# Hybrid block on one core: the compressed branch's transposition first in each group, its product behind the first unit

## The chip, the cores and the metric

The kernel runs on one NeuronCore of a Trainium2 chip. The metric is the device time of one execution in microseconds (us). Below, TensorE is the matrix engine (PE in the trace, with PEld for its weight loads), ScalarE is ACT, VectorE is DVE, GpSimd is POOL, SyncE is SP.

## What is computed

One transformer block of 512 tokens and width 1024: an mLSTM branch and a sparse attention branch side by side, then an output projection, a convolutional feed-forward part, a gated embedding and a last norm. The change lies in the sparse attention, where each query takes the gated sum of three softmax branches:

```python
# per group g of 4 heads, per block of queries
s_c = einsum(q, Kc) - slope * dist_c;  p_c = softmax(s_c)      # compressed keys: 31 of them
o_c = einsum(p_c, Vc)
o_s = einsum(softmax(q Ksel - ...), Vsel)                      # selected blocks: all 512 positions
o_w = einsum(softmax(q Kwin - ...), Vwin)                      # window: all 512 positions
return g0 * o_c + g1 * o_s + g2 * o_w
```

The sums over keys may be taken in any order, so the compressed branch may come anywhere among the others.

## The kernel before

Every product of two float32 matrices is made of three in a faster form: a value is split into a rounded part and the rest (hi and lo), and hi*hi, lo*hi and hi*lo are added in PSUM.

The attention stage runs over eight *groups* (g, i): g is one of two sets of four heads, i one of four blocks of 128 queries, in the order (0,3), (0,2), (0,1), (0,0), (1,0), (1,1), (1,2), (1,3). `scores` (lines 698 to 756) makes, for one head, the scores on TensorE (tile s), their exponentials on ScalarE (line 747) and the gated probabilities on VectorE and GpSimd (lines 755 and 753). For the two long branches they stand in E, queries by keys; for the compressed branch the four heads of a group share Ec, 128 queries by 4 x 32 keys.

A group's values are worked off in *units* (`value_units`, line 758): one for each 128 keys of a long branch, so 2(i+1), and one for the compressed branch. `CPOS` = (1, 2, 2, 2) (line 32) sets the place of the latter: second in the groups with i = 0, third in the others. The main loop (lines 814 to 843) does for each unit:

- `value_turn`: TensorE turns the probabilities of the four heads into a PSUM tile pt, keys by queries (line 780: four transpositions of 128 x 128). ScalarE copies it into ph, the hi part (line 783), and VectorE takes the rest into pl (line 784). pt, ph and pl have two buffers each.
- For the compressed unit there is one transposition (line 771), since the four heads lie side by side in Ec. Its outcome has head r in rows 32r to 32r+31, so four ScalarE copies of 32 x 128 (line 774) bring the heads side by side into rows 0 to 31 of the one tile phc, and four VectorE subtractions of 32 x 128 (line 777) put the rest into rows 32 to 63.
- The products of the unit *before* (`value_product`): two of 128 x 512 (lines 788 and 790) into the group's sum pv, or for the compressed unit a single one, of phc (line 788 too).
- Scores of the next group, one head after another, and `st.fill(FILL1)`: 0.9 us, by the plan's own estimates, of *filler*, which is a projection that needs nothing of the attention (pmo, pmq: 24 products of 128 x 512 each; later poa, the output projection).

Behind a group's last product `value_end` copies half of pv on ScalarE (os, line 794), adds the halves on VectorE (ao, line 797), and splits the sum into mixa (lines 803 and 804). The output projection poa (lines 411, 412, 415) multiplies mixa; its first two of four input blocks are group set g = 0, the others g = 1.

`st.spend` only moves the plan's clock, by which a few later steps are put in. The text order is not the last word: a scheduler reorders the instructions of each engine by its own estimates when the program is built, and the engines then run their queues strictly in that order.

Of the kernel before, what the change touches and what calls it, by code (L numbers as in the profile page):

```python
# [11 lines left out]
AF = mybir.ActivationFunctionType  # L12
# [16 lines left out]
T_GATES = 8.0  # L29
T_CT = 8  # L30
T_CS = 3.0
CPOS = (1, 2, 2, 2)
NSC = (0, 2)
HO = (2, 2, 2, 3)
T_NS = 3.2
# [26 lines left out]
def f32(ap):  # L62
    return ap.bitcast(F32)
# [3 lines left out]
def hybrid_block_kernel(ctx: ExitStack, tc: tile.TileContext, a, out):  # L67
    nc = tc.nc
    TE, VE, SE, GE = nc.tensor, nc.vector, nc.scalar, nc.gpsimd
# [8 lines left out]
    def bank(tag, bufs, n, name):  # L78
        shape = [128, 512] if n == 1 else [128, n, 512]
        return psum.tile(shape, F32, tag=tag, bufs=bufs, name=name)  # L80
# [10 lines left out]
    def pT(name):  # L91
        return bank("T", 2, 1, name)

    def pV(name):
        return bank("V", 1, 1, name)
# [137 lines left out]
    st = Stream()  # L233
# [3 lines left out]
    ident, negm = cols[:, C_ID:C_ID + 128], cols[:, C_NEG:C_NEG + 128]  # L237
# [109 lines left out]
    def first_split(k):  # L347
        g = xbuf[:, k, S:S + 1]
        SE.activation(xh[:, k], xbuf[:, k, 0:S], AF.Copy, scale=g)
        raw = s1raw[min(k, k // 2 * 2) if k > 1 else k]  # L350
        raw = raw[:, k % 2 if k > 1 else 0]
        for c0, c1 in (((0, 288), (288, W1)) if k == 0 else ((0, W1),)):
            i = SE.activation(hi1[:, k % 6, c0:c1], raw[:, c0:c1], AF.Copy)
        VE.scalar_tensor_tensor(xl[:, k], xbuf[:, k, 0:S], g, f32(xh[:, k]), op0=ALU.mult, op1=ALU.subtract)
        for c0, c1 in (((0, 288), (288, W1)) if k == 0 else ((0, W1),)):
            VE.tensor_sub(lo1[:, k % 6, c0:c1], raw[:, c0:c1], f32(hi1[:, k % 6, c0:c1]))
        return i
# [10 lines left out]
    for k in range(KB):  # L368
        last = first_split(k)
# [58 lines left out]
    Vc = apool.tile([128, 2, 128], F32R, name="Vc")  # L428
    phc = apool.tile([128, 512], F32R, name="phc")
# [266 lines left out]
    Ec = {}  # L696
# [61 lines left out]
    def value_units(g, i):  # L758
        n = (i + 1) * 128
        units = []  # L760
        for br in range(2):
            for kt in range(i + 1):
                units.append((br * n + kt * 128, V[:, kt, 2 * br + g]))
        units.insert(CPOS[i], (None, Vc[:, g]))
        return units

    def value_turn(g, i, Es, u, unit):
        c0, vs = unit
        pt = pT(f"pt{g}{i}_{u}")
        if c0 is None:  # L770
            TE.transpose(pt[:, 0:128], Ec.pop((g, i)).rearrange("p r n -> p (r n)"), ident)
            for r in range(4):
                src, sl = pt[32 * r:32 * r + 32, 0:128], slice(r * 128, (r + 1) * 128)
                SE.activation(phc[0:32, sl], src, AF.Copy)
            for r in range(4):
                src, sl = pt[32 * r:32 * r + 32, 0:128], slice(r * 128, (r + 1) * 128)
                VE.tensor_sub(phc[32:64, sl], src, f32(phc[0:32, sl]))
            return phc, None
        for r in range(4):
            TE.transpose(pt[:, r * 128:(r + 1) * 128], Es[r][:, c0:c0 + 128], ident)  # L780
        ph = main.tile([128, 512], F32R, tag="PH", bufs=2, name=f"ph{g}{i}_{u}")
        pl = main.tile([128, 512], F32R, tag="PL", bufs=2, name=f"pl{g}{i}_{u}")
        SE.activation(ph, pt, AF.Copy)  # L783
        VE.tensor_sub(pl, pt, f32(ph))  # L784
        return ph, pl

    def value_product(pv, vs, ph, pl, first, last):
        TE.matmul(pv, vs, ph, start=first, stop=False)  # L788
        if pl is not None:
            TE.matmul(pv, vs, pl, start=False, stop=last)  # L790

    def value_end(g, i, pv):
        os = t2k(f"os{g}{i}")
        SE.activation(os[0:64], pv[64:128], AF.Copy)
        ao = t2k(f"ao{g}{i}")
        for par in range(2):
            VE.tensor_add(ao[par * 64:(par + 1) * 64, 0:256].rearrange("p (b n) -> p b n", b=2),
                          pv[0:64].rearrange("p (b o n) -> p o b n", b=2, o=2)[:, par],
                          os[0:64].rearrange("p (b o n) -> p o b n", b=2, o=2)[:, par])
        aov = ao[:, 0:256].rearrange("p (b n) -> p b n", b=2)  # L800
        dh = mixa[:, 0, 2 * g:2 * g + 2, i * 128:(i + 1) * 128]
        dl = mixa[:, 1, 2 * g:2 * g + 2, i * 128:(i + 1) * 128]
        SE.activation(dh, aov, AF.Copy)
        VE.tensor_sub(dl, aov, f32(dh))
# [9 lines left out]
    for x, (g, i) in enumerate(groups):  # L814
        nxt = groups[x + 1] if x + 1 < len(groups) else None
        if nxt and nxt[0] != g:
            st.until("q11")
        units = value_units(g, i)
        nu = len(units)
        pv = None  # L820
        Ns = []
        for u in range(nu):
            got = value_turn(g, i, Es, u, units[u])
            st.spend(0.43)
            if pend:
                pend()
                st.spend(0.43)
            if u == 0:
                pv = pV(f"pv{g}{i}")

            def product(u=u, got=got, g=g, i=i, pv=pv, vs=units[u][1], last=(u == nu - 1)):
                value_product(pv, vs, *got, u == 0, last)
                if last:
                    value_end(g, i, pv)
            pend = product
            if nxt:
                while len(Ns) * nu < 4 * (u + 1):
                    st.fill(FILL0)
                    Ns.append(scores(*nxt, len(Ns)))
                    st.spend(score_cost[nxt[1]])  # L840
            st.fill(FILL1)
        Es = Ns
# [488 lines left out]
```

## Time and profile before

| | us |
|---|---|
| median of 3 runs (lowest, highest) | 641.08 (640.48, 641.81) |
| the profiled execution | 639.04 |
| its span, first to last instruction | 637.2 |
| TensorE busy in the span | 618.9 |
| VectorE busy | 426.6 |
| ScalarE busy | 314.1 |
| attention's value stage, about 103 to 244 us | 141 |

The profile gives one execution: for every instruction its engine, its start and how long it was under way, and for every idle stretch which instruction ended it. Products on TensorE overlap: one of 128 x 512 is shown as 0.39 us long, while the next starts 0.23 us after it. A wait thus shows as idle time only from 0.16 us up; by the starts it is seen whole.

### The profile page before, as it was taken

The numbers are of one execution on the slowest core, as the hardware profiler recorded it, in microseconds if no ns is written. First come the engines' busy times: TensorE is split into PE (matmuls) and PEld (weight loads), VectorE is DVE, ScalarE is ACT, GpSimd is POOL, SyncE is SP. The second block draws the span as 40 slices with busy tenths as digits, with TensorE's granted clock in tenths as the row PEclk, the third lists the DMA queues.
The fourth block names the chain that finished last, engine by engine and source line by source line (L and its number), as shares of the span: only waits on it lengthen the run. The fifth ranks groups of instructions, "written<-read, shape, count | busy, mean of one in ns | idle before, by whom it ended". The sixth has DMA issues, their size and how long they took to land. (4 is left out here: it accounts for less than half of the span.)

```text
span 637.2 us, 8437 instructions
## 1 busy us (share of the span) xinstructions
PE 618.9 (97%) x3013; PEld 498.4 (78%) x3013; DVE 426.6 (67%) x882; ACT 314.1 (49%) x656; POOL 36.6 (6%) x85
## 2 busy tenths in 40 slices
PE   9997999999999999999999999999999999999994
PEld 6886877777777777777878888888888888888884
DVE  6898648888878977784786555565656444445476
ACT  7457445677656756555555334343333323233254
POOL 0400005211111200000000000000000000000000
PEclk9999999999999999999999999999999999999999
DMA  8702034211121153013233333333222233534703
GB/s 327 288 22 96 14 120 121 79 34 38 63 67 33 34 199 99 34 34 99 67 99 100 100 99 100 99 100 97 93 88 93 93 100 100 143 120 135 195 3 133
DMA packets 22921, 63.02 MB, mean 99 GB/s; under 512 B 2712, under 2 KB 7192, under 8 KB 22812
## 3 DMA queue, kind: packets, MB, share of 16 engines
q1 hardware_dynamic: 21344, 59.92, 28.8%
q0 software_dynamic: 1248, 2.16, 1.5%
q8 instruction: 24, 0.39, 0.3%
q10 hardware_dynamic: 288, 0.41, 0.2%
q14 instruction: 17, 0.14, 0.1%
HBM read 56.71 MB, written 2.10 MB: 92 GB/s over the span
## 5 line engine op out<-in xcount | busy, mean ns | idle before, releaser
L1080 ACT ACTIVATE u<-zv 128x512 fp32r<-128x512 f32 x16 | 10.1, 633 | 45.3 <-DVE zv L1078 45.3
L1077 DVE TENSOR_TENSOR zv<-pu,n2rb 128x512 f32<-128x512 f32 x16 | 11.1, 691 | 31.3 <-PE pu L415 31.3
L783 ACT ACTIVATE ph<-pt 128x512 fp32r<-128x512 f32 x40 | 23.5, 598 | 16.9 <-PE pt L780 16.3
L784 DVE TENSOR_TENSOR pl<-pt,ph 128x512 fp32r<-128x512 f32 x40 | 27.0, 684 | 6.6 <-ACT ph L783 6.0
L753 POOL TENSOR_SCALAR E<-E,rr 128x512 f32<-128x512 f32 (+3 forms) x32 | 21.2, 663 | 158.1 <-DVE rr L750 111.8
L1067 DVE TENSOR_TENSOR zg<-pu,n2rb 128x512 f32<-128x512 f32 x16 | 11.1, 692 | 26.0 <-PE pu L415 24.6
L780 PE MATMUL pt<-cols,E 128*128 128x128 f32 x160 | 27.7, 274 | 0.4 <-DVE E L755 0.3
L780 PEld LDWEIGHTS pt<-cols,E 128*128 128x128 f32 x160 | 20.0, 140 | 7.1 <-DVE E L755 2.6
L1107 DVE TENSOR_TENSOR X<-pd,X 128x512 f32<-128x512 f32 x8 | 5.5, 692 | 29.6 <-PE pd L415 29.6
L1070 ACT ACTIVATE cv<-zg,cols 128x512 f32<-128x512 f32 x16 | 13.1, 816 | 20.1 <-DVE zg L1067 20.1
L1073 ACT ACTIVATE cv<-cv 128x512 f32<-128x512 f32 x16 | 10.1, 631 | 24.6 <-DVE cv L1072 24.6
L747 ACT ACTIVATE E<-s,nm 128x384 f32<-128x384 f32 (+2 forms) x48 | 22.2, 473 | 0.0
L788 PE MATMUL pv<-ph,V 128*128 128x512 f32 x40 | 18.7, 468 | 0.4 <-ACT ph L783 0.4
L1081 DVE TENSOR_TENSOR u<-zv,u 128x512 fp32r<-128x512 f32 x16 | 11.1, 692 | 10.5 <-ACT u L1080 10.5
L790 PE MATMUL pv<-pl,V 128*128 128x512 f32 x40 | 16.7, 416 | 0.0
L737 DVE TENSOR_REDUCE nm<-s 128x2 f32<-128x768 f32 (+2 forms) x24 | 16.3, 681 | 0.0
L1066 POOL MEMSET zg<- 128x2 f32 x16 | 1.5, 100 | 244.0 <-DVE cv L1072 151.0
L261 DVE TENSOR_TENSOR acc<-acc,sq 128x512 f32<-128x512 f32 x21 | 14.4, 684 | 0.1
L964 PEld LDWEIGHTS mo<-vo,mw 128*128 128x128 f32 x80 | 11.4, 191 | 2.1 <-issue 0.7
L755 DVE TENSOR_SCALAR E<-E,rr 128x512 f32<-128x512 f32 (+3 forms) x32 | 13.0, 405 | 0.1
L749 DVE RECIPROCAL rr<-rs 128x3 f32<-128x3 f32 x32 | 5.5, 171 | 11.1 <-ACT E L747 11.1
L747 ACT ACTIVATE Ec<-s,nm 128x32 f32<-128x32 f32 x24 | 6.9, 286 | 11.8 <-DVE nm L737 11.6
(1102 smaller groups left out, 2017.6 us busy)
## 6 DMA issues: line engine op xcount, KB each, us to landing
X<-in_xg SPq DMA_DIRECT2D x1, 2048.0 KB, 8.5
xo<-xturn SPq DMA_DIRECT2D x32, 64.0 KB, 2.1
wgr<-in_w_pg SPq DMA_DIRECT2D x4, 512.0 KB, 4.6
s1r<-in_w_s SPq DMA_DIRECT2D x3, 672.0 KB, 9.2
xT<-in_xg SPq DMA_DIRECT2D x3, 514.0 KB, 8.3
rawx<-in_cmp_w SPq DMA_DIRECT2D x3, 512.0 KB, 6.2
Q<-hlq POOLq DMA_DIRECT2D x12, 128.0 KB, 3.3
out_y<-xo SPq DMA_DIRECT2D x3, 512.0 KB, 2.6
```

Source lines behind the costliest of these rows:

```text
L261: return VE.tensor_add(acc[:, :n], acc[:, :n], sq[:, :n])
L737: VE.tensor_reduce(out=nm[:, 1:3], in_=sw, axis=AX.X, op=ALU.max, negate=True)
L747: SE.activation(e, p, AF.Exp, bias=nm[:, b:b + 1], accum_out=rs[:, b:b + 1])
L753: GE.tensor_scalar(e, e, rr[:, b:b + 1], 0.0, op0=ALU.mult, op1=ALU.add)
L755: VE.tensor_scalar(e, e, rr[:, b:b + 1], None, op0=ALU.mult)
L780: TE.transpose(pt[:, r * 128:(r + 1) * 128], Es[r][:, c0:c0 + 128], ident)
L783: SE.activation(ph, pt, AF.Copy)
L784: VE.tensor_sub(pl, pt, f32(ph))
L788: TE.matmul(pv, vs, ph, start=first, stop=False)
L790: TE.matmul(pv, vs, pl, start=False, stop=last)
L964: TE.matmul(po[:, 0:130], Ws[j][:, (i - j) * 128:(i - j + 1) * 128], vones(j, h), start=(j == 0), stop=(j == i))
L1070: SE.activation(cv, zg[:, 2:S + 2], AF.Identity, scale=cw(2), bias=cols[:, C_CB + f:C_CB + f + 1])
```

## The change

The compressed branch is no unit any more. `CPOS` and its unit are gone, so a group has one unit fewer. A new step, `c_turn`, does its transposition, its four copies and its four subtractions ahead of the group's first unit. The one product of phc with Vc follows the first unit's two products. No instruction is added, dropped or altered in size; the plan's clock is moved by 0.11 and 0.23 us for the moved steps, and eight `st.fill(FILL1)` fall away in the text, so that filler is taken later.

```diff
-CPOS = (1, 2, 2, 2)
...
-        units.insert(CPOS[i], (None, Vc[:, g]))
         return units
+
+    def c_turn(g, i):
+        pt = pT(f"pt{g}{i}_c")
+        TE.transpose(pt[:, 0:128], Ec.pop((g, i)).rearrange("p r n -> p (r n)"), ident)
+        for r in range(4):
+            src, sl = pt[32 * r:32 * r + 32, 0:128], slice(r * 128, (r + 1) * 128)
+            SE.activation(phc[0:32, sl], src, AF.Copy)
+        for r in range(4):
+            src, sl = pt[32 * r:32 * r + 32, 0:128], slice(r * 128, (r + 1) * 128)
+            VE.tensor_sub(phc[32:64, sl], src, f32(phc[0:32, sl]))
...
-        if c0 is None:
-            TE.transpose(pt[:, 0:128], Ec.pop((g, i)).rearrange("p r n -> p (r n)"), ident)
...
-            return phc, None
...
+        c_turn(g, i)
+        st.spend(0.11)
         for u in range(nu):
             got = value_turn(g, i, Es, u, units[u])
...
                 value_product(pv, vs, *got, u == 0, last)
+                if u == 0:
+                    TE.matmul(pv, Vc[:, g], phc, start=False, stop=False)
+                    st.spend(0.23)
```

What becomes of the engines' queues, at the two places that matter. In the names, pt01_0 is unit 0 of group (0,1), pt01_c the compressed transposition, E2_1 the probabilities of head 2 in query block 1.

TensorE at the start of group (0,1), before:

```order
L780 MATMUL pt01_0_1558<-cols_73,E0_1_1364 128x128
L780 MATMUL pt01_0_1558<-cols_73,E1_1_1413 128x128
L780 MATMUL pt01_0_1558<-cols_73,E2_1_1466 128x128
L411 MATMUL pmo3_1538<-x1h_119,mo3h_1383 128x512
L412 MATMUL pmo3_1538<-x1l_120,mo3h_1383 128x512
L788 MATMUL pv02_1351<-ph02_6_1548,V_309 128x512
L780 MATMUL pt01_0_1558<-cols_73,E3_1_1518 128x128
L730 MATMUL s0_0_1580<-K_308,Q0_560 128x320
L732 MATMUL s0_0_1580<-K_308,Q0_560 128x320
L734 LDWEIGHTS identb_114
L734 MATMUL s0_0_1580<-maskt_115,identb_114 128x2x128
L790 MATMUL pv02_1351<-pl02_6_1549,V_309 128x512
```

and with the change, from the compressed transposition to the group's first product:

```order
L767 MATMUL pt01_c_1540<-cols_73,Ec01_1372 128x128
L779 MATMUL pt01_0_1550<-cols_73,E0_1_1370 128x128
L779 MATMUL pt01_0_1550<-cols_73,E1_1_1409 128x128
L779 MATMUL pt01_0_1550<-cols_73,E2_1_1471 128x128
L779 MATMUL pt01_0_1550<-cols_73,E3_1_1509 128x128
L411 MATMUL pmo3_1597<-x1l_120,mo3h_1426 128x512
L410 MATMUL pmo3_1597<-x1h_119,mo3h_1426 128x512
L411 MATMUL pmo3_1597<-x1l_120,mo3h_1426 128x512
L410 MATMUL pmo3_1597<-x1h_119,mo3h_1426 128x512
L787 MATMUL pv01_1568<-ph01_0_1555,V_309 128x512
```

The transpositions of unit 0 were spread over the end of the group ahead; now all five stand together behind it, four filler products follow, and then the first product, which needs ph01_0. Groups (0,3), (1,2) and (1,3) have the same five and four filler products; (1,0) has a mask product more; (1,1) has three fillers, a score product and two masks; (0,2) five fillers and two masks; (0,0) eight fillers.

ScalarE at the same place, before:

```order
L747 ACTIVATE E3_1_1518,rs3_1_1519<-s3_1_1509,nm3_1_1508 128x256 x2
L577 ACTIVATE vo_886<-vo_886 128x512
L783 ACTIVATE ph02_6_1548<-pt02_6_1543 128x512
L783 ACTIVATE ph01_0_1563<-pt01_0_1558 128x512
L794 ACTIVATE os02_1569<-pv02_1351 64x512
```

and with the change:

```order
L792 ACTIVATE os02_1561<-pv02_1358 64x512
L576 ACTIVATE vo_886<-vo_886 128x512
L770 ACTIVATE phc_311<-pt01_c_1540 32x128 x4
L782 ACTIVATE ph01_0_1555<-pt01_0_1550 128x512
L801 ACTIVATE mixa_885<-ao02_1563 128x2x128
```

The four copies of the compressed part now stand ahead of ph01_0, and that holds in all eight groups; before, it was so only in (1,0), with three of the four.

TensorE at the end of the stage, group (1,3), before:

```order
L788 MATMUL pv13_2456<-ph13_7_2565,V_309 128x512
L790 MATMUL pv13_2456<-pl13_7_2566,V_309 128x512
L415 MATMUL pmq7_2627<-x1h_119,mq7l_2578 128x512 x3
L788 MATMUL pv13_2456<-ph13_8_2589,V_309 128x512
L935 MATMUL pb0_2671<-gmr_314,sel4_117 128x512
L955 MATMUL ms00_2686<-qk_1839 128x512
L790 MATMUL pv13_2456<-pl13_8_2590,V_309 128x512
L411 MATMUL poa0_2703<-mixa_885,woa0h_2693 128x512
L412 MATMUL poa0_2703<-mixa_885,woa0h_2693 128x512
L411 MATMUL poa0_2703<-mixa_885,woa0h_2693 128x512
L412 MATMUL poa0_2703<-mixa_885,woa0h_2693 128x512
L411 MATMUL poa1_2722<-mixa_885,woa0h_2693 128x512
```

and with the change:

```order
L787 MATMUL pv13_2430<-ph13_6_2524,V_309 128x512
L410 MATMUL poa1_2722<-mixa_885,woa0h_2693 128x512
L411 MATMUL poa1_2722<-mixa_885,woa0h_2693 128x512
L788 MATMUL pv13_2430<-pl13_6_2525,V_309 128x512
L787 MATMUL pv13_2430<-ph13_7_2539,V_309 128x512
L788 MATMUL pv13_2430<-pl13_7_2540,V_309 128x512
L410 MATMUL poa0_2703<-mixa_885,woa0h_2693 128x512
L410 MATMUL poa1_2722<-mixa_885,woa0h_2693 128x512
L411 MATMUL poa0_2703<-mixa_885,woa0h_2693 128x512
L410 MATMUL poa0_2703<-mixa_885,woa0h_2693 128x512
L411 MATMUL poa0_2703<-mixa_885,woa0h_2693 128x512
```

Before, eight products on the first two input blocks of poa0 and poa1 stood between the stage's last product and the first one that reads the mixa of group (1,3); now they stand further up, between the products of group (1,3), as do pb0 and ms00.

## Rows read from the trace of the kernel before

**Rows 1.** The page, busy time, share of the span and instructions.

```profile
PE 618.9 (97%) x3013; PEld 498.4 (78%) x3013; DVE 426.6 (67%) x882; ACT 314.1 (49%) x656; POOL 36.6 (6%) x85
```

**Rows 2.** Stretches of the stage: width, busy time (instructions) per engine, PEclk, DMA share, GB/s.

```profile
103.00:241.20 138.20, 135.33 (x716) 104.22 (x715) 113.00 (x303) 92.30 (x281) 23.06 (x38) 1.00 0.24 73
241.20:244.04 2.84, 2.63 (x11) 1.65 (x9) 2.48 (x5) 1.34 (x3) 0.00 (x0) 1.00 0.13 20
```

**Rows 3.** Waits of TensorE, 103 to 245 us: us in total, times, longest.

```profile
PE pv L788 <- DVE phc L777: 1.3, 3, 0.6
PE s L730 <- ACT E L747: 0.5, 1, 0.5
PE pv L788 <- ACT ph L783: 0.4, 1, 0.4
PE pt L780 <- DVE E L755: 0.3, 1, 0.3
PE poa L411 <- ACT mixa L803: 0.2, 1, 0.2
```

**Rows 4.** Tile phc: duration in ns min/median/max, first and last start.

```profile
L774 ACT ACTIVATE phc<-pt x32: 250/270/274, 113.1 to 230.7; 32x128 fp32r<-32x128 f32 x32
L777 DVE TENSOR_TENSOR phc<-pt,phc x32: 279/285/295, 114.6 to 231.9; 32x128 fp32r<-32x128 f32 x32
```

**Rows 5.** TensorE in order of time, group (1,0): start us, us, instruction [idle before].

```profile
176.37 0.27 PE L771 MATMUL pt<-cols,Ec 128*128 128x128 f32 x1
...
177.52 0.39 PE L411 MATMUL pmq<-x1h,mq2h 128*128 128x512 f32 x1
178.27 0.50 PE L788 MATMUL pv<-ph,V 128*128 128x512 f32 x1 [0.37 <-ACT ph L783]
178.61 0.40 PE L412 MATMUL pmq<-x1l,mq2h 128*128 128x512 f32 x1
```

**Rows 6.** ScalarE in order of time, groups (1,0) and (1,3).

```profile
176.74 0.86 ACT L774 ACTIVATE phc<-pt 32x128 fp32r<-32x128 f32 x3 [2.84 <-PE pt L771]
177.62 0.60 ACT L783 ACTIVATE ph<-pt 128x512 fp32r<-128x512 f32 x1
...
229.89 1.11 ACT L774 ACTIVATE phc<-pt 32x128 fp32r<-32x128 f32 x4 [1.12 <-PE pt L771]
231.03 0.60 ACT L783 ACTIVATE ph<-pt 128x512 fp32r<-128x512 f32 x1
```

**Rows 7.** TensorE in order of time, group (1,3), four transpositions and the fillers behind.

```profile
230.17 0.60 PE L780 MATMUL pt<-cols,E 128*128 128x128 f32 x4
230.52 0.48 PE L411 MATMUL pmq<-x1h,mq7h 128*128 128x512 f32 x1
230.84 0.39 PE L412 MATMUL pmq<-x1l,mq7h 128*128 128x512 f32 x1
```

**Rows 8.** ScalarE in order of time, group (0,1), compressed copies and the exponentials behind.

```profile
151.99 1.11 ACT L774 ACTIVATE phc<-pt 32x128 fp32r<-32x128 f32 x4 [0.32 <-PE pt L771]
...
153.75 0.37 ACT L747 ACTIVATE E<-s,nm 128x128 f32<-128x128 f32 x1
```

**Rows 9.** TensorE, then ScalarE and VectorE, at the end of the stage.

```profile
241.18 0.79 PE L790 MATMUL pv<-pl,V 128*128 128x512 f32 x1
241.81 0.39 PE L411 MATMUL poa<-mixa,woa0h 128*128 128x512 f32 x1
...
243.43 0.40 PE L412 MATMUL poa<-mixa,woa0h 128*128 128x512 f32 x1
244.04 0.73 PE L411 MATMUL poa<-mixa,woa0h 128*128 128x512 f32 x2 [0.21 <-ACT mixa L803]
...
242.01 0.59 ACT L794 ACTIVATE os<-pv 64x512 f32<-64x512 f32 x1 [0.49 <-PE pv L790]
...
239.96 0.69 DVE L784 TENSOR_TENSOR pl<-pt,ph 128x512 fp32r<-128x512 f32 x1 [0.77 <-ACT ph L783]
```

**Rows 10.** VectorE in order of time, group (1,3), the compressed subtractions.

```profile
231.04 1.18 DVE L777 TENSOR_TENSOR phc<-pt,phc 32x128 fp32r<-32x128 f32 x4 [1.44 <-ACT phc L774]
```

More of the change, by code (lines that the diff above doesn't have):

```diff
@@ L769, in value_turn @@
         pt = pT(f"pt{g}{i}_{u}")
-        if c0 is None:
-            TE.transpose(pt[:, 0:128], Ec.pop((g, i)).rearrange("p r n -> p (r n)"), ident)
[L772 to L777, printed above, removed]
-            return phc, None
         for r in range(4):
@@ L788, in value_product @@
         TE.matmul(pv, vs, ph, start=first, stop=False)
-        if pl is not None:
-            TE.matmul(pv, vs, pl, start=False, stop=last)
+        TE.matmul(pv, vs, pl, start=False, stop=last)
     def value_end(g, i, pv):
```

## The prediction

> **What bounds the kernel now.** The page comes first: TensorE is busy for 97% of the span, ScalarE for 49% [rows 1]. The table of stretches narrows this to the value stage: of 138.2 us TensorE is shown busy for 135.3 at the full granted clock (PEclk 1.00), and of the last 2.84 us for 2.63 [rows 2]. No instruction is added or dropped, so TensorE's own work stays what it is and the change can only move TensorE's waits. The list of waits is therefore the next view: in this stage it holds five entries, 2.5 us together, and the largest is the one that the change is about, three waits for phc, 1.3 us [rows 3]. Then the stretches of the timeline around the compressed unit show how long its steps take on each engine.
>
> Idle time understates a wait. A product of 128 x 512 is shown 0.39 us long and the next one starts 0.23 us behind it [rows 7, 9], so 0.16 us of each wait is hidden under the product ahead. The product behind a wait also hands over late: 178.27 to 178.61 is 0.34 us where the step is 0.23 [rows 5], about 0.1 more. I count a listed wait as its idle time plus 0.26 us.
>
> **What goes.** The three waits for phc: the new product of phc stands behind the first unit's two, and on VectorE the four subtractions into phc stand ahead of that unit's pl, which is worked off in order. Whoever has pl has phc. So 1.3 + 3 x 0.26 = 2.1 us go [rows 3]. The wait for E (0.3 us idle, at the start of group (0,2)) goes, since that group's transpositions now stand behind a score block: 0.3 + 0.26 = 0.6 us [rows 3]. The wait of a score product for ScalarE (0.5 us) was in group (0,1): the exponentials it waited for stood behind the four compressed copies, 151.99 to 153.1 [rows 3, 8]. Those copies are elsewhere now, and the 1.1 us they took is more than the wait: 0.5 + 0.26 = 0.7 us after rounding. Together 3.4 us go.
>
> **What comes, at the start of each group.** This is the largest term. ScalarE copies phc in four pieces ahead of ph of unit 0, and TensorE can't make the group's first product before that ph. Before, one group had nearly this order already, (1,0), with three of the four copies ahead, and TensorE waited there: the compressed transposition starts at 176.37, the three copies at 176.74, ph at 177.62, the first product at 178.27 with 0.37 us of idle time [rows 5, 6]. That is 1.90 us from the transposition to the first product. Three copies took 0.88 us, four take 1.14 (229.89 to 231.03) [rows 6], so with the fourth it is 1.90 + 0.26 = 2.16 us.
>
> What TensorE has to do meanwhile is in the new order: five transpositions and, in four groups, four fillers. Four transpositions take 0.35 us (230.17 to 230.52), so 0.11 more for the fifth, 0.46; the first filler behind them takes 0.32, the others 0.23 each [rows 7], 1.01. That is 1.47 us, and the wait is 2.16 - 1.47 = 0.69 us in each of (0,3), (0,1), (1,2) and (1,3). Groups (1,0) and (1,1) have a mask product or a score block and one filler fewer: I take 0.63 us for each. (0,2) has a filler and two masks more: 0.69 - 0.23 - 0.1 = 0.35 us. (0,0) has four fillers more, 0.92 us, which covers it: 0. Sum 4 x 0.69 + 2 x 0.63 + 0.35 = 4.4 us, and 7 x 0.1 = 0.7 us for the late hand-over. Less the wait of (1,0) that was there before, 0.37 + 0.26 = 0.6 us, it is 4.5 us.
>
> This supposes that ScalarE is free when the compressed transposition lands. Where it still has a copy of half a group sum (0.59 us, the os of [rows 9]) or of a weight ahead, the wait grows. In (0,0), (0,2) and (1,1) such a step stands just ahead in the new queue. I take nothing for it and keep 3 x 0.6 = 1.8 us for the upper end. The lower end is copies that hand over at once, at their own shortest duration of 0.25 us [rows 4] where their starts lie 0.285 apart: 4 x 0.035 = 0.14 us less in each of seven groups, 1.0 us less.
>
> [...] The starts in the trace lie 0.285 us apart, and ph takes 0.60 us [rows 6]. [...]
>
> **What comes, on VectorE.** The four subtractions, 1.18 us [rows 10], now lie between ph and pl of unit 0. They start when the fourth copy is done, together with ph, so pl of unit 0 is there at about 0.37 + 1.14 + 1.18 + 0.69 + 0.1 = 3.5 us after the compressed transposition [rows 6, 9, 10]. In the tightest groups, (1,1) and (1,3), TensorE has the first product, three fillers and four transpositions ahead of it: 2.16 + 0.33 + 0.23 x 2 + 0.46 + 0.32 = 3.7 us. The cover is 0.2 us thin. I cost it at nothing; if VectorE comes 0.2 to 0.4 us late in these and two other groups, up to 0.8 us are added.
>
> **What comes, at the end of the stage.** With one unit fewer in each group, and the filler placed otherwise, the last projection runs out early, and the first eight products of the output projection are drawn into group (1,3). Before, they covered the way from the group's sum to mixa. That way is shown whole: the last product of pv ends at 241.18 + 0.79 = 241.97, os starts at 242.01, and the first product that reads the new mixa starts at 244.04: 2.07 us [rows 9]. The product ahead of that one starts at 243.43, so the wait was 0.61 - 0.23 = 0.38 us. Now nothing stands between, and TensorE is free 0.16 us before the last product's shown end: 2.07 + 0.16 = 2.23 us. That is 1.85 us more. The eight products could give it back inside group (1,3) only if TensorE waited there; but apart from the wait for phc, which is already taken off, the list shows no wait in it [rows 3], and the transpositions and products there were covered by filler of the same kind. So all of it is counted.
>
> The group's last unit loses its cover too. ph and pl of unit 7 are now multiplied one directly behind the other, where pb0 and ms00 stood between before. pl comes 0.69 us after ph [rows 9] and the product of ph takes 0.3: 0.4 us.
>
> **Sum.** 4.5 + 1.85 + 0.4 - 3.4 = 3.3 us more. The profiled execution took 639.04 us, 1.8 us of it outside the span; with the change it would be 642.4. The median of the runs lies 2.0 us above the profiled execution, so the forecast against the median is 641.08 + 3.3 = 644.4 us, 0.5% slower.
>
> **Rivals.**
> - *Queues ahead are late.* ScalarE is still busy at the start of three groups (1.8 us) and VectorE's cover fails (0.8 us): 644.4 + 2.6 = 647.0 us. For it: ScalarE's weight copies and os stand right ahead of phc in the new queue. Against it: ScalarE is idle for half of the time [rows 1]. 0.14.
> - *The moved products pay.* TensorE would have waited in group (1,3), since the projection has run out, and the eight products fill just that (1.85 us back); with copies at their shortest (1.0 us back) the sum is 3.3 - 2.85 = 0.45, so 641.5 us, no change. Against it: the waits in rows 3 show nothing to fill there. 0.12.
> - *The first wait is covered, and the kernel is faster.* If the copies run into each other, the term of 4.5 us vanishes. That is so when four of them take less than 1.14 - 0.69 = 0.45 us, or when seven or more fillers stand behind the five transpositions, as in (0,0). Then 3.4 + 0.6 us go, 1.85 + 0.4 come, and it is 641.08 - 1.8 = 639.3 us. Against it: one copy is never under 0.25 us [rows 4], and the wait at 178.27 is this very wait. 0.06.
> - *It doesn't do what it says.* The products of phc still wait. VectorE's order excludes it unless pl of the first unit waits in its place, which would cost the 2.1 us again: 646.5 us. 0.03.
>
> **Chances.** The forecast has 0.65, with a range of its own from 643.0 to 646.0. What a measurement of this kernel can tell from no change is about 0.2%, 1.3 us. Slower by more than that is the forecast, the late queues and the fourth rival, 0.65 + 0.14 + 0.03 = 0.82; within it 0.12; faster 0.06. The range, 641.8 to 646.8, leaves out the faster case, the lower half of the second rival and the upper half of the late queues: 0.06 + 0.06 + 0.07 = 0.19.
>
> **What would show it.** Right: the list of waits no longer has phc, and has ph with seven or eight waits of 0.4 to 0.7 us idle at the groups' first products; the wait of poa for mixa is about 2 us; each group's four copies and ph follow each other without a gap on ScalarE. Wrong: ph waits under 0.2 us, a wait of pl at the first unit that outweighs them, or a wait for mixa that stays near 0.2.

## The result, and the profile after

| | before | after |
|---|---|---|
| median, us (lowest to highest; runs) | 641.34 (640.48 to 641.81; 4) | 645.25 (644.34 to 645.81; 4) |
| ratio, 95% interval | | 1.0069 (1.0052 to 1.0086) |
| the profiled execution | 639.04 | 645.6 |
| its span; mean granted clock of TensorE | 637.2; 0.998 | 643.6; 0.988 |

The change makes the kernel 3.9 us slower, 0.7%; the forecast was 644.4 us, 3.3 us slower. On the page TensorE is busy for longer [rows 1], with the same instructions, and the row of granted clocks (tenths, 40 slices of 16 us) has dips that the busy shares don't explain:

```profile
PE 623.3 (97%) x3013; PEld 503.4 (78%) x3013; DVE 427.1 (66%) x882; ACT 314.9 (49%) x656; POOL 36.1 (6%) x85
...
PEclk9999899999999998999999999999999999999998
```

The list of TensorE's waits from 102 to 252 us goes beside [rows 3] (us in total, times, longest). phc is gone, as are the waits for E. In their place stand eight waits for ph, one in each group, and the wait for mixa: 5.6 us of idle time where there were 2.7.

```profile
PE pv L787 <- ACT ph L782: 3.4, 8, 0.7
PE poa L410 <- ACT mixa L801: 2.0, 1, 2.0
PE pv L788 <- DVE pl L783: 0.2, 1, 0.2
```

Group (1,0) in order of time, TensorE and then ScalarE, beside [rows 5, 6]. The transposition at 178.12 is followed by four copies and then ph, without a gap on ScalarE, and the first product comes 2.47 us behind the transposition:

```profile
178.12 0.27 PE L767 MATMUL pt_c<-cols,Ec 128*128 128x128 f32 x1
178.24 0.60 PE L779 MATMUL pt<-cols,E 128*128 128x128 f32 x4
...
180.59 0.50 PE L787 MATMUL pv<-ph,V 128*128 128x512 f32 x1 [0.72 <-ACT ph L782]
...
178.77 1.15 ACT L770 ACTIVATE phc<-pt_c 32x128 fp32r<-32x128 f32 x4 [2.67 <-PE pt L779]
179.94 0.60 ACT L782 ACTIVATE ph<-pt 128x512 fp32r<-128x512 f32 x1
```

Group (0,0), ScalarE and the first product. Here the copies themselves start late, because a weight's copy of 1.06 us is ahead of them in the queue:

```profile
164.02 1.06 ACT L147 ACTIVATE mq2h<-mq2r 128x1024 fp32r<-128x1024 f32 x1 [1.94 <-PE pmq L411]
164.98 1.13 ACT L770 ACTIVATE phc<-pt_c 32x128 fp32r<-32x128 f32 x4
166.14 0.60 ACT L782 ACTIVATE ph<-pt 128x512 fp32r<-128x512 f32 x1
...
166.79 0.50 PE L787 MATMUL pv<-ph,V 128*128 128x512 f32 x1 [0.43 <-ACT ph L782]
```

Group (1,3), TensorE up to its first product, the shortest of the eight waits:

```profile
233.14 0.30 PE L767 MATMUL pt_c<-cols,Ec 128*128 128x128 f32 x1
233.28 0.85 PE L779 MATMUL pt<-cols,E 128*128 128x128 f32 x4
233.89 1.17 PE L414 MATMUL pmq<-x1h,mq7l 128*128 128x512 f32 x4
235.27 0.50 PE L787 MATMUL pv<-ph,V 128*128 128x512 f32 x1 [0.20 <-ACT ph L782]
```

The end of the stage, beside [rows 9]. TensorE stands idle for 2.0 us, and behind that the products of 128 x 512 step by 0.43 us instead of 0.23:

```profile
246.60 0.50 PE L788 MATMUL pv<-pl,V 128*128 128x512 f32 x1 [0.18 <-DVE pl L783]
249.10 1.09 PE L410 MATMUL poa<-mixa,woa0h 128*128 128x512 f32 x2 [2.01 <-ACT mixa L801]
250.00 0.63 PE L411 MATMUL poa<-mixa,woa0h 128*128 128x512 f32 x1
250.42 0.63 PE L410 MATMUL poa<-mixa,woa0h 128*128 128x512 f32 x1
```

Stretches (width, busy time and instructions of each engine, then PEclk, DMA share, GB/s): two of them ran at half the clock (0.50), what lies between at the full one (1.00).

```profile
62.30:68.20 5.90, 5.90 (x14) 4.64 (x15) 5.58 (x9) 3.86 (x7) 0.00 (x0) 0.50 0.01 3
68.40:249.00 180.60, 175.02 (x934) 136.54 (x932) 136.13 (x349) 109.83 (x317) 26.97 (x44) 1.00 0.25 76
249.30:252.60 3.30, 3.30 (x9) 2.49 (x9) 1.05 (x3) 2.47 (x7) 0.00 (x0) 0.50 0.00 0
```

The first of these stretches goes with a wait of 2.8 us ahead of pmv (one of the earlier projections), in code that the change doesn't touch. The profiled execution of before has the same wait and the full clock behind it. The wait after, the wait before, and the stretch around it before:

```profile
62.22 0.79 PE L327 MATMUL pmv<-mv0h,x1h 128*128 128x512 f32 x1 [2.76 <-ACT mv0h L147]
62.34 0.50 PE L328 MATMUL pmv<-mv0h,x1h 128*128 128x512 f32 x1 [2.76 <-ACT mv0h L148]
59.50:66.40 6.90, 4.14 (x20) 3.30 (x18) 6.71 (x10) 5.32 (x8) 0.00 (x0) 1.00 0.23 78
```

So spans can't be compared as they are. What can be compared is the *stretch* from the first row of s_3a (scores of the first group) to the first product of ppp: both lie behind the first half clock, and the same products stand between them. Its two ends, after and then before:

```profile
93.53 0.42 PE L729 MATMUL s_3a<-K,Q 128*128 128x272 f32 x2
289.66 0.39 PE L911 MATMUL ppp<-pp0h,phl 128*128 128x512 f32 x1
```

```profile
90.75 0.42 PE L730 MATMUL s_3a<-K,Q 128*128 128x272 f32 x2
283.38 0.39 PE L908 MATMUL ppp<-pp0h,phl 128*128 128x512 f32 x1
```

That is 196.13 us against 192.63, 3.5 us more. Two questions are left: which of the waits make it, and what the clock costs.

### The profile page after: what moved, and what is told of

It is laid out like the page before. It is cut to its first block, busy times and chain, and to the rows that moved or that the text cites. A ratio compares the mean times of both kernels' runs of the same rounds, so it can differ in the third digit from the quotient of the medians.

```text
span 643.6 us, 8451 instructions
## 1 busy us (share of the span) xinstructions
PE 623.3 (97%) x3013; PEld 503.4 (78%) x3013; DVE 427.1 (66%) x882; ACT 314.9 (49%) x656; POOL 36.1 (6%) x85
## 3 DMA queue, kind: packets, MB, share of 16 engines
q0 software_dynamic: 1248, 2.16, 1.5%
## 5 line engine op out<-in xcount | busy, mean ns | idle before, releaser
L779 PE MATMUL pt<-cols,E 128*128 128x128 f32 x160 | 24.8, 273 | 0.1
L770 ACT ACTIVATE phc<-pt_c 32x128 fp32r<-32x128 f32 x32 | 8.6, 268 | 10.3 <-PE pt_c L767 7.2
L787 PEld LDWEIGHTS pv<-ph,V 128*128 128x128 f32 x40 | 7.5, 188 | 7.6 <-ACT ph L782 7.3
L773 DVE TENSOR_TENSOR phc<-pt_c,phc 32x128 fp32r<-32x128 f32 x32 | 9.1, 286 | 6.5 <-ACT phc L770 5.9
```

## The experiments

All in one table: the stretch of the profiled execution, the median of all runs, and the ratio to the kernel before that ran beside it (its medians: 641.1 to 641.3 us). e2 to e16 are names of kernels; what each of them changes is said below.

| kernel | stretch, us | median, us | ratio, 95% |
|---|---|---|---|
| before | 192.63 | 641.1 to 641.3 | |
| after | 196.13 | 645.25 | 1.0069 (1.0052 to 1.0086) |
| e2, after with one copy | 190.86 | 638.94 | 0.9962 (0.9948 to 0.9976) |
| e13, before with one copy | 190.71 | 638.65 | 0.9967 (0.9953 to 0.9982) |
| e3, product back | 194.28 | 644.27 | 1.0045 (1.0028 to 1.0062) |
| e8, copies later | 195.91 | 645.16 | 1.0062 (1.0045 to 1.0079) |
| e16, copies later, mended | 193.08 | 641.61 | 1.0010 (0.9998 to 1.0023) |
| e4, eight products held back | 194.71 | 643.11 | 1.0029 (1.0017 to 1.0041) |
| e5, wait for mixa filled | 194.92 | 643.02 | 1.0031 (1.0019 to 1.0043) |
| e10, both waits filled | 194.84 | 642.22 | 1.0019 (1.0008 to 1.0030) |
| e6, before, first wait filled | 192.73 | 638.82 | 0.9966 (0.9954 to 0.9978) |
| e11, e2 and first wait filled | 190.69 | 636.74 | 0.9936 (0.9920 to 0.9952) |
| e12, one move | 191.13 | 637.83 | 0.9953 (0.9935 to 0.9970) |
| e14, one move, late | 190.26 | 636.88 | 0.9934 (0.9921 to 0.9948) |

**Are the copies the cause?** Take three of the four away, in the new order and in the old. The subtractions stay, so for three heads the whole value goes into the second half of phc.

```diff
-        for r in range(4):
+        for r in range(1):
             src, sl = pt[32 * r:32 * r + 32, 0:128], slice(r * 128, (r + 1) * 128)
             SE.activation(phc[0:32, sl], src, AF.Copy)
```

> The changed kernel with one of the four ScalarE copies of phc instead of four; three quarters of the compressed values' first half are left out. Three copies lie 0.86 us apart from first to last, more than the 0.37 to 0.89 us that each group's first product is late behind ph in the changed kernel. Theory (the copies ahead of ph make that wait): the eight waits for ph, 3.4 us of idle time and 4.8 us of lost steps, go down to under 1.5 us lost, and 641 us or less is left of 645.25. In this build the last projection's products stand at the end of the stage again, so the wait for mixa and the half clock behind it go as well, some 3 us; with both it is 638.5 to 640.5. Rival (the wait comes from the first unit's place behind the scores, not from the copies): ph waits stay at 0.3 to 0.6 us idle in seven groups, and only the end is better, 642 to 643.

> The kernel before with one of the four ScalarE copies of phc (for three heads the second half of phc takes the whole value, unsplit): with it and the changed kernel with one copy (638.94 us) the two orders stand side by side with and without the copies. Theory (the copies' place is all that the change costs): without them the orders are equal, so 638 to 640 us, a difference to 638.94 of under 1 us against 4.1 with four copies. Rival (the order costs by itself, in the last group's filler and its end): 637.5 us or less, with the change still 1.5 us or more slower.

Waits of TensorE with one copy, 102 to 252 us, new order and then old:

```profile
PE pt_c L767 <- DVE Ec L754: 0.3, 1, 0.3
PE pt L779 <- DVE phc L773: 0.3, 1, 0.3
PE poa L411 <- DVE mixa L802: 0.3, 1, 0.3
```

```profile
PE pv L788 <- DVE phc L777: 1.1, 2, 0.8
PE pt L780 <- DVE E L755: 0.3, 1, 0.3
```

All eight waits for ph are gone, and the two orders are equal: 638.94 and 638.65 us, stretches 0.15 us apart. With four copies they are 3.5 apart. So the whole cost of the new order comes about through the four copies. That takes in the end of the stage: in e2 eight products of poa stand there again, and the wait for mixa and the half clock behind it are gone too, so this pair doesn't say what the copies cost inside the groups alone. And the copies cost the kernel before too: 1.9 us of its stretch.

**Or their place?** The product of phc alone goes back to where it was:

```diff
-                if u == 0:
+                if u == (0, 1, 1, 1)[i]:
                     TE.matmul(pv, Vc[:, g], phc, start=False, stop=False)
```

> The changed kernel with only the product of phc back where it was, behind the second unit's pair in the groups of four to eight units; the transposition and the copies stay first. Theory (the cost is in the copies' place; the product of phc waits for nothing at either place): the same eight waits for ph, 3.4 us idle, no wait for phc, 644.5 to 646 us. Rival (the product behind the first pair is part of the cost, as it shifts filler away from the next unit): 643 us or less.

Its list has 2.7 us for ph in six waits and 1.6 us for mixa, and the clock stays full (stretch behind the wait, below). So the waits for ph stay with the copies, but they are not "the same eight": they are 0.7 us less. The median, 644.27 us, is just under the expected range; the stretch is 1.85 us shorter than after's. With the 0.7 us go 0.4 us less of the wait for mixa and the half clock (1.2 us, below); these three make more than 1.85 us, and how they share it isn't shown. The place of the product is a part of the cost after all, in the main through the end of the stage.

```profile
PE pv L787 <- ACT ph L782: 2.7, 6, 0.7
PE poa L410 <- ACT mixa L801: 1.6, 1, 1.6
```

```profile
249.20:252.60 3.40, 3.36 (x13) 2.26 (x14) 1.53 (x4) 2.47 (x7) 0.00 (x0) 1.00 0.01 4
```

Then the whole compressed step goes one unit back, its product one unit behind it:

```diff
-        c_turn(g, i)
-        st.spend(0.11)
         for u in range(nu):
             got = value_turn(g, i, Es, u, units[u])
             st.spend(0.43)
+            if u == min(1, nu - 2):
+                c_turn(g, i)
+                st.spend(0.11)
             if pend:
...
-                value_product(pv, vs, *got, u == 0, last)
-                if u == 0:
+                if u == min(2, nu - 1):
                     TE.matmul(pv, Vc[:, g], phc, start=False, stop=False)
                     st.spend(0.23)
+                value_product(pv, vs, *got, u == 0, last)
```

> The changed kernel, with the compressed transposition, its four copies and its four subtractions moved behind the second unit's ph (behind the first unit's in groups of two units), and the product of phc one unit behind that. All the work is there; only the place differs. Theory (the eight waits for ph come from the copies standing ahead of the first ph of a group): first products find ph ready, the waits for ph fall from 3.4 us idle to under 1.2, and phc is not waited for, since a whole unit lies between; the order at the end of the stage is the same as in the changed kernel, so the 2.0 us wait for mixa and the half clock behind it stay. 645.25 - 3 = about 642 us. Rival (the copies cost the same wherever they stand, since they only move to the next ph): 644.5 to 645.5 us.

In this kernel the edit also changes the computation. A group's last product is made in the loop of the next group and there reads that group's number of units: so the product of phc in (1,0) is left out, and (0,0) takes its successor's phc. Its time went the rival's way, 645.16 us. The waits for ph are gone, but others came, and behind the wait for mixa the clock is halved as in after:

```profile
PE poa L410 <- ACT mixa L801: 2.0, 1, 2.0
PE pt L779 <- DVE phc L773: 0.8, 2, 0.6
PE pt L779 <- DVE pl L783: 0.4, 1, 0.4
```

```profile
248.70:252.00 3.30, 3.30 (x8) 2.62 (x9) 1.08 (x3) 2.47 (x7) 0.00 (x0) 0.50 0.00 0
```

A transposition now waits for VectorE's subtractions into phc, which hold one of the two buffers of pt. In e16 the step stands behind the open product instead of ahead of it, and every group has its own number of units (against e8, the line of `product` shortened):

```diff
-            if u == min(1, nu - 2):
-                c_turn(g, i)
-                st.spend(0.11)
             if pend:
                 pend()
                 st.spend(0.43)
+            if u == min(1, nu - 2):
+                c_turn(g, i)
+                st.spend(0.11)
...
-            def product(..., last=(u == nu - 1)):
+            def product(..., last=(u == nu - 1), nu=nu):
```

> The whole computation with the four copies as in the changed kernel, but the compressed transposition, its copies and its subtractions behind the second unit's turn and behind the product that stood open (the first unit's in groups of two), and the product of phc one unit later, ahead of that unit's pair. Unlike in e8, every group's product is taken with its own values, and the end of the stage has four products of the output projection ahead of the new mixa again. Theory (first place in the group is the worst place for the copies; later they lie beside more work of TensorE): ph waits at the groups' first products are gone, the wait for mixa is under 1.2 us and the clock doesn't halve there, and it is 641 to 642.5 us, as before. Rival (four copies cost the same at each place that isn't free by itself, as e8 seemed to say): 643.5 to 645 us.

```profile
PE poa L410 <- ACT mixa L801: 1.1, 1, 1.1
PE pt L779 <- DVE phc L773: 1.0, 2, 0.5
PE pt L779 <- DVE E L754: 0.4, 2, 0.2
```

That is the theory's side: 641.61 us, the same as before. What divides e8 and e16 is in the main the end, 0.9 us of the wait for mixa and 1.2 for the half clock (below), 2.1 of 2.8 us.

Inside the groups both kernels have 1.8 us of listed idle time where after has 3.6, and yet e8's stretch is only 0.2 us shorter than after's. Where did e8's saving go? A wait of under 0.15 us of idle time isn't listed. By the starts it is seen, as here in the trace of before, where the score product comes 0.53 us behind the filler, 0.3 us late:

```profile
165.94 0.40 PE L411 MATMUL pmq<-x1h,mq1h 128*128 128x512 f32 x1
166.47 0.42 PE L730 MATMUL s<-K,Q 128*128 128x320 f32 x1
```

An estimate over the whole stretch goes by all steps of TensorE from one start to the next. From each step it takes off the usual step for the same three shapes one behind the other (the value that a fifth of such steps in all these profiles lie below); what is left is lateness. Against after, the steps that end in a listed wait have 2.4 us less of it in e8, and all other steps have 2.1 us more. So what e8 saved came back as waits too short for the list. Taking the copies out of first place bought nothing there, since the 0.2 us of stretch are about the one product that is left out. In e16 it bought some 0.9 us inside the groups (3.05 us of stretch, less the 2.1 of the end); the rest came through the end.

**What is the end worth?** In e4 the eight products that moved into (1,3) are held behind the last product of pv, as they stood before (`floor` is that product, given for poa alone; m1 and m2 are the products of a block with hi and lo of mixa):

```diff
...
+            if floor is not None:
+                behind(m1, floor, "pv first")
+                behind(m2, floor, "pv first")
...
```

> The changed kernel, but the eight products of the output projection that had moved into group (1,3) are held behind the last product of pv, where the kernel before had them. Theory of the prediction (they fill nothing inside the group, and 1.85 us at its end): the wait for mixa falls from 2.0 us idle to under 0.4, the half clock of 3.4 us behind it goes too, and the time falls by 1.9 + 1.3 to about 642 us. Rival (the moved products pay inside the group): ph to pl of units 3 to 7 is bare without them, 0.69 us of VectorE against 0.23 of one product and 0.46 of transpositions, so four or five waits for pl of 0.2 to 0.5 us come, together 1.5 to 2 us, only the half clock is won back, and it is 643.5 to 644.5 us.

```profile
PE pv L791 <- ACT ph L786: 3.4, 8, 0.7
PE pv L792 <- DVE pl L787: 1.0, 3, 0.6
PE poa L410 <- ACT mixa L805: 0.2, 1, 0.2
```

```profile
247.40:252.60 5.20, 5.03 (x21) 3.48 (x21) 3.33 (x7) 2.94 (x9) 0.00 (x0) 1.00 0.00 0
```

In e5 they stay, and the wait is filled with nine products that count for nothing:

```diff
+NKEEP = 9
...
+    pwarm = pT("pwarm")
+    for _ in range(NKEEP):
+        k = TE.matmul(pwarm, identb, maskt[:, None, :].to_broadcast([128, 4, 128]), start=True, stop=True)
+        behind(k, pvlast[0], "keep")
```

> The changed kernel with nine products of two constants into an unused bank between the last product of pv and the first that reads the new mixa: nothing of the kernel's work moves, and TensorE is busy in the wait of 2.0 us. Theory (the half clock of 249.28 to 252.69 us comes from that idle time, and costs apart from it): the clock stays full there, the products behind step 0.23 us and not 0.43, and the time falls by 1.2 to 1.7 us to about 643.8 us. Rival (the clock would have fallen there anyway, or the wait hides it): still half, or full and without a gain, 645 to 645.5 us.

```profile
247.10:249.20 2.10, 2.08 (x10) 0.77 (x9) 1.27 (x3) 1.01 (x2) 0.00 (x0) 1.00 0.00 0
249.20:252.60 3.40, 3.36 (x13) 2.26 (x14) 1.53 (x4) 2.48 (x7) 0.00 (x0) 1.00 0.00 0
```

With TensorE busy, the clock stays full, and the stretch is 1.2 us shorter, although no work of the kernel starts earlier for it: the first product that reads the new mixa starts 155.57 us behind the start of the stretch in after and 155.66 in e5. So here the idle time brings the half clock, and the half clock costs 1.2 us on its own. The medians differ by 2.2 us, but that isn't the price of the end alone: in after's profile the half clock at pmv lasts 6.8 us, in e5's 3.4.

e4 has the full clock too and is no faster than e5 (643.11 and 643.02 us). Of the 1.8 us of idle time that it saves ahead of mixa, 0.8 come back in the list as waits for pl inside the group, and by the estimate above some 0.7 more as steps too short to list. Its median lies between the two forecasts, but the rival's mechanism was right: holding the products back is worth 0.2 us of stretch, not 1.9.

**What is left without the clock?** The wait ahead of pmv is filled in the same way, in the kernel before (e6), in after together with e5's edit (e10), and in e2 (e11):

```diff
+NKEEP0 = 11
...
                 ps.extend(four("pmv"))
+                for _ in range(NKEEP0):
+                    TE.matmul(ps[0], identb, maskt[:, None, :].to_broadcast([128, 4, 128]), start=True, stop=True)
```

> The kernel before with eleven products of two constants in TensorE's wait of 2.8 us ahead of the first product of pmv (59.5 to 62.3 us), into the bank that this product starts afresh. Theory (most executions of both kernels run at half the clock for some 7 us behind that idle time, as the profiled one of the changed kernel does, and the profiled one of before doesn't, which is why it is 2 us under its median): with TensorE busy there, all executions have the full clock, and the median falls from 641.3 by 2.3 to 2.8 us to 638.5 to 639. Rival (that stretch belongs to the changed kernel, or to single executions): before has it rarely, its median stays at 641 to 641.6, and 2.8 us of the 3.9 between the kernels are this stretch and not the waits.

```profile
59.50:68.00 8.50, 8.13 (x44) 5.43 (x42) 8.25 (x12) 5.32 (x8) 0.00 (x0) 1.00 0.20 64
```

> The changed kernel with both fillings: eleven products of two constants in the wait of 2.8 us ahead of pmv, and nine in the wait of 2.0 us for mixa. With the half clock gone from both places what is left against the kernel before with the first filling (638.8 us) is the waits of the change alone. Theory (of the 3.9 us between the kernels the waits are 2.1 to 2.3 and the half clock behind the wait for mixa is 1.6 to 1.8): 645.25 - 2.2 - 2.3 = 640.8 us, between 640.5 and 641.2, and the profile shows the full clock from the first tile to the last. Rival (the two savings overlap, or the first stretch is met less often in the changed kernel): 641.5 to 643 us.

> The changed kernel with one of the four ScalarE copies of phc (for the other three heads the second half of phc then takes the whole value, unsplit) and the eleven products in the wait ahead of pmv. Theory (the two savings are independent, 6.3 us from the copies and the end, 2.3 us from the clock at the start; the one-copy kernel's profile has half the clock for 3.4 us there): 638.9 - 1.5 to 2.3 = 636.6 to 637.4 us. Rival (once the copies are gone, that stretch costs nothing any more, since something else is late): 638.5 to 639 us.

e6 came as the theory had it: 638.82 us, 2.3 under the kernel before beside it, eleven of twelve runs from 638.48 to 639.18. That is where before's profile stood all along, since its execution happened to have the full clock. e6's stretch is before's (192.73 and 192.63 us), so the filling sped up nothing but what stands right behind that wait. e11 takes the same 2.2 us off e2. e10 missed: 642.22 us where 640.5 to 641.2 was expected. The time is the rival's, but not its reasons: e10's profile has the full clock from pmv to ppp, and all four runs of after have a mean clock of 0.988 to 0.990, so none of them was without half clocks. Its stretch is as the theory had it (2.1 us over e6's), but the profiled execution is 2.8 us longer than e6's and the median 3.4. 0.7 us of that lies behind the first product of pu, in code that is the same in all these kernels and in which TensorE's last product starts 308.8 to 309.7 us later in their profiles. The rest of the miss is open, and with it what the change costs outside the stretch.

**A version that beats both.** One ScalarE copy and one VectorE subtraction of the whole 128 x 128, and eight small DMAs on POOL's queue that bring the pieces into phc; e6's filling is in it as well.

```diff
...
+        hl = t2k(f"hlc{g}{i}", F32R)[:, 0:256].rearrange("p (a q) -> p a q", a=2)
+        SE.activation(hl[:, 0], pt[:, 0:128], AF.Copy)
+        VE.tensor_sub(hl[:, 1], pt[:, 0:128], f32(hl[:, 0]))
         for r in range(4):
+            for a_ in range(2):
+                move(phc[32 * a_:32 * a_ + 32, r * 128:(r + 1) * 128], hl[32 * r:32 * r + 32, a_])
...
```

> All of the computation is there: the compressed transposition stands behind the first unit's turn, ScalarE copies its 128 x 128 once, VectorE subtracts once, and eight small DMAs on POOL's queue put the pieces into phc, whose product is taken ahead of the third unit's (the second's in groups of two); and the eleven products ahead of pmv. Theory (what costs is the string of four small steps on ScalarE and on VectorE, whatever their place): with one step on each, 636.5 to 637.5 us, as with one copy left. Rival (the DMAs land too late, about 3.3 us behind their issue where Q's do in the trace of before, or their eight issues of 0.54 us hold up POOL's scaling of E): waits for phc or E of 2 us and more in sum, 639 us or more.

Between e12 and e14 only the product's place differs, and that each group's own number of units counts (the line of `product` shortened):

```diff
-            def product(..., last=(u == nu - 1)):
-                if u == min(2, nu - 1):
+            def product(..., last=(u == nu - 1), nu=nu):
+                if u == min(3, nu - 1):
```

> The whole computation, in the form of e12 (one ScalarE copy and one VectorE subtraction of 128 x 128 for each group, eight small DMAs on POOL's queue into phc, eleven products ahead of pmv), with every group's product of phc taken, and taken one unit later, ahead of the fourth unit's pair (the second's in groups of two), since in e12 two products waited 1.6 us for the DMA. Theory (the string of small steps on ScalarE and VectorE is what costs, and one unit more covers the DMA): the waits for phc fall under 0.5 us, and it is 636.5 to 637.8 us, faster than both kernels and than the kernel before with the filled wait (638.8). Rival (POOL's queue delays the DMAs behind its own scaling whatever the product's place): waits for phc of 1.5 us and more stay, and it is 638 us or more.

In e12 the product of phc of group (1,0) is left out, as in e8; two of the others waited 1.6 us for the DMAs, and its 637.83 us lie between theory and rival. e14 has all of the computation: 636.88 us, 4.3 us or 0.66% faster than the kernel before. Of these 2.3 are the filled wait (e6), and some 2 come from the new compressed step; its shorter string and its later place aren't told apart here. One wait of 1.0 us for the DMA is left; what was expected was under 0.5. Tile hlc (duration in ns min/median/max):

```profile
L772 ACT ACTIVATE hlc<-pt_c x8: 270/276/278, 109.8 to 223.0; 128x128 fp32r<-128x128 f32 x8
L773 DVE TENSOR_TENSOR hlc<-pt_c,hlc x8: 275/280/292, 110.2 to 223.3; 128x128 fp32r<-128x128 f32 x8
```

The copy of 128 x 128 takes about as long as each of the four of 32 x 128 did: by the medians 0.276 us for 128 rows at once, against 4 x 0.270 us for four times 32 [rows 4].

## Why the prediction was right, and where it wasn't

The time, its sign and the main mechanism came as forecast, and the listed waits came to nearly the forecast sum. But the sum left out two things that nearly cancel, and that they do is luck: waits too short to be listed became fewer, by some 1.3 us, and the half clock at the end cost 1.2 us. Between the ends of the stretch the change costs 3.5 us, and 2.1 without the half clock (e10 against e6).

- *phc's waits go*: right, none is listed, and the order is no worse elsewhere on VectorE: the first unit's pl, costed at nothing, isn't waited for.
- *The wait for ph, seven groups, 4.4 us*: eight groups, 3.4 us idle, which with 0.16 for each is 4.7. Group by group it was less good. (0,0) was put at nothing and has 0.43 us idle, because the weight's copy stands ahead on ScalarE, as the rival of the late queues had it. In (1,0) ScalarE began 0.65 us behind the transposition and not 0.37, so 0.72 us idle. In (1,3) only 0.20 is idle: the way from transposition to product is 2.13 us, as forecast (2.16), but TensorE had 1.76 us of work in it and not 1.47, in the main because the four transpositions took 0.61 us (233.28 to 233.89) and not 0.35.
- *A listed wait costs its idle time and 0.26 us, and nothing else moves*: the second half of this step failed. By the estimate from the starts, the steps that end in a listed wait are 3.9 us too long in e6, and in e10 5.1 us and 2.3 more for the wait for mixa, which is filled there: 3.4 us more, where the forecast's sum is 3.3. But all other steps together became some 1.3 us shorter, and the stretch grew by 2.1. The largest part of that is score products that stood waiting behind filler, as at 166.47 above: 0.8 us too long in e6, 0.3 in e10. The prediction counted only what the list shows.
- *The end*: 2.23 us was forecast for the wait for mixa, 2.27 came (246.60 to 249.10, less 0.23); for the last pl 0.4, and 0.35 came (246.02 to 246.60, less 0.23). The sentence that the eight moved products fill nothing is wrong in the new order: held back, in e4, they win 0.2 us. They stand where mq7's products stood before, which are used up earlier now. That the drawing forward of filler to the groups' starts is what costs, and that it only shows at the end, is argued from the order and not shown.
- *The clock* was the step left out. The prediction saw the wait of 2 us coming and priced it at its own length. The trace of before has no product at half the clock, so nothing there gave the price; but its median stood 2.0 us above its profile, and e6 shows that this was the clock.
- *The rivals*: of the late queues one group's part came true; the moved products pay inside the group, though not against the kernel before.
- *A sum*: the five waits of [rows 3] are 2.7 us together and not 2.5. Nothing else rests on it.

## What to carry to other kernels

Here a string of small copies on a side engine cost time where the bound engine had little other work to cover it, and each move chose who waits: products of phc before, each group's first product after, transpositions in e8 and e16. Shortening the string, from four copies to one, paid in both orders: 1.9 us of stretch in the old one (e13 against before) and 5.3 in the new (e2 against after, with the end in it). Filler is a stock: what covers a new wait at one place can be missing at the next. A list of waits leaves out the short ones, and a change can move waits across that line: compare starts too. When a wait of about 2 us on TensorE is foreseen, ask what the clock does behind it (here, behind 2.0 us, it was halved for 3.4 us in after), and compare executions from points that lie behind such stretches.

## What was not expected of the hardware

- TensorE's clock. Behind 2.0 us idle (for mixa) the granted clock was 0.50 for 3.4 us in both profiles with that wait (after, e8); behind 1.6 us (e3) and 1.1 us (e16) it stayed at 1.00. With the wait of 2.8 us (for pmv) it differed from one execution to the next: 1.00 in the profile of before, 0.50 for 3.4 us in those of e2 to e5, e13 and e16, for 6.8 us in those of after and e8. In steps of 0.2 us over the whole traces of before and after it was 0.50 or 1.00, but for six steps at the changes.
- Runs of one kernel differ by it: of 35 runs of the kernel before, four had a mean clock of 0.997 and took 639.0 to 639.8 us, and five had 0.990 and took 641.7 to 642.5. With the wait filled, eleven of twelve lay within 0.7 us.
- Products that count for nothing, put into a wait, made a kernel faster: e6, by 0.34%.
